# A hybrid attention layer on one core: other priorities and PSUM banks in the handover to the feed-forward, a shorter Newton step, and a last product in two column halves

## The chip, the cores and the metric

The kernel runs on one core of one Trainium2 chip. The metric is device time in microseconds (us) of one execution, from its start to its end. The engines are named as in the profile: PE is TensorE (matrix products and transposes), PEld its weight loads, DVE is VectorE, ACT is ScalarE, POOL is GpSimd and SP is SyncE, which here only issues transfers (DMA). PSUM is the memory into which PE writes its results; it has eight banks of 128 partitions by 512 fp32 columns.

## The reference

One decoder layer on 512 rows of 1024 columns, and a last normalisation, all in fp32:

```python
def rmsnorm(x, w):
    return x * lax.rsqrt(jnp.mean(x * x, axis=-1, keepdims=True) + EPS) * w

h = rmsnorm(x, norm1_w)
proj = h @ w_in                                  # split among three head groups
mix = concat(dilated_attention(...), gla(...), moba_attention(...))      # (512, 1024)
x = x + mix @ w_out
h2 = rmsnorm(x, norm2_w)
x = x + jnp.square(jax.nn.relu(h2 @ w_ff1)) @ w_ff2          # 1024 -> 4096 -> 1024
out = rmsnorm(x, final_norm_w)
```

The change begins where `x + mix @ w_out` has been formed and ends with the output.

## The kernel before

**Precision.** An fp32 matrix is held as a high part and a low part of a format that PE multiplies fast (`wh` and `wl` of a weight, `mh` and `ml` of `mix`, `yp` twice for the activations, `Ah` and `Al` for the hidden values). A product takes three matrix instructions: high by high, low by high, high by low. ACT makes a high part by a copy, DVE the low part by a subtraction. Weights arrive as `wraw` (512 KB a piece) and are split into `wh` and `wl`.

**Output projection** (`out_proj`). The rows are four tiles t = 0 to 3 of 128, the columns two halves of 512. Tiles 0 and 2 add up in the PSUM banks "mm", tiles 1 and 3 in "s" (tile name `ops`). As a half is done, `x2_out` adds it to `x` on DVE, ACT squares it with a running sum (`junk`, `ssq`), and DVE puts the sum into `m`. After the second half `inv_rms` works out 1/sqrt(m): ACT takes a logarithm and an exponential (both named `y` in the profile) and one Newton step on DVE refines the result (`tmp`, `tmp`, `y`). `y_out` scales each half (`y0`, shown as `y` of 128x512), PE transposes it into a bank (`yps`, four 128x128 transposes a half), and ACT or DVE copies it out with the norm's weights as scale (`yf`).

**Feed-forward** (`ffn`). The 4096 hidden columns are four chunks c. For each chunk the first layer (`f1...`) and the second (`f2...`) are each done as seven block products instead of eight (n = 0, 1, 3, 5, 2, 4, 6 in this order, in banks named X, Y and Z), whose operands are sums and differences of blocks: `y_parts` forms those of the activations (`ys`, then the high and low `yp`), `a_parts` those of the hidden values, and the weights' are formed by accumulating loads on POOL's queue or on DVE. The transposes of tiles 2 and 3 lie among the first chunk's products, since n = 0 and n = 1 need tiles 0 and 1 only.

**The end.** The last unit of work is the second layer of chunk 3, and its last product n = 6, for q = 0 (row tile t = 2) and then q = 1 (t = 3). `add` adds a product to `x`, `square_sum` and `final` normalise: the half that came last is written as `of` (DVE), the other half was multiplied with the final weights `fw` ahead of time on POOL (`xw`) and is only scaled by ACT. All output transfers are issued by SP.

**What sets the order.** The program is recorded by a planner (`Plan`). Each piece of work is a stream with a priority. The planner holds an estimated cost for every operation and picks again and again the operation that could start first, and among equals the stream with the lowest priority number; streams wait for each other's events (`wait`, `fire`) and for resources such as banks (`take`, `give`). Each engine then runs its operations in the order of these picks. All instructions are issued by one line, L129 of the kernel, so the profile tells them apart by tile names and not by lines.

Of the kernel before, what the change touches and what calls it, by code (L numbers as in the profile page):

```python
# [199 lines left out]
def hybrid_block_kernel(ctx: ExitStack, tc: tile.TileContext, xT_d, x_d, w0_d, wv_d, wqk_d, wo_d, w1_d, w2_d,  # L200
# [13 lines left out]
    def slot(name, dt=F32, shape=(128, 512)):  # L214
        return sp.tile(list(shape), dt, name=name, tag="slot", bufs=SLOTS)
# [20 lines left out]


    nw = consts.tile([128, 2, KT], F32)
    hsel = consts.tile([128, 4], F32)
    bav = consts.tile([128, 1], F32)  # L240
    ones = consts.tile([128, 128], F32)
# [696 lines left out]
        return slot(name, dt, (128, 2, 256))  # L938
    ssq = {}

    def square_sum(t, half):

        q = small("ssq", (128, 1))
        second = t in ssq
        if not second:
            ssq[t] = small("m", (128, 1))
        yield ACT.activation(slot("junk"), x3[t, half], AF.Square, accum_out=q)
        if second:
            yield ("wait", ("ssq0", t))
            plan.done.pop(("ssq0", t))  # L950
            yield DVE.scalar_tensor_tensor(ssq[t], q, 1.0 / D, ssq[t], op0=OP.mult, op1=OP.add)
            fire(("ssq", t))
        else:
            yield DVE.tensor_scalar(ssq[t], q, 1.0 / D, EPS, op0=OP.mult, op1=OP.add)
            fire(("ssq0", t))

    def inv_rms(t):
        yield ("wait", ("ssq", t))
        plan.done.pop(("ssq", t))
        m = ssq.pop(t)  # L960
        y, tmp = (small(x, (128, 1)) for x in ("y", "tmp"))
        yield from rsqrt(y, m, tmp)
        st["inv", t] = y

    def x2_out(t, half, acc, r):
        yield DVE.tensor_tensor(x3[t, half], acc, x3[t, half], op=OP.add)
        give(r)
        yield from square_sum(t, half)
        if half:
            yield from inv_rms(t)  # L970
            y = st.pop(("inv", t))
            for hf in range(2):
                spawn(y_out(t, hf, y), 1)

    def y_out(t, half, y):
        y0 = slot("y0")
        yield Any(DVE.tensor_scalar(y0, x3[t, half], y, None, op0=OP.mult), ACT.activation(y0, x3[t, half], AF.Copy, scale=y))
        yield ("take", "pt")
        pt = bank("pt", "yps")
        yield [PE.transpose(pt[:, i * 128:(i + 1) * 128], y0[:, i * 128:(i + 1) * 128], ident) for i in range(4)]  # L980
        ts = slice(t % 2 * 128, t % 2 * 128 + 128)
        ks = range(half * 4, half * 4 + 4)
        src = [pt[:, i * 128:(i + 1) * 128] for i in range(4)]
        if t % 2 == 0:
            yf[half, t // 2] = [new("yf") for _ in range(2)]
        else:
            yield ("wait", ("yf", t - 1, half))
        for i, k in enumerate(ks):
            out, scale = yf[half, t // 2][i // 2][:, i % 2, ts], nw[:, 1, k:k + 1]
            yield Any(ACT.activation(out, src[i], AF.Copy, scale=scale), DVE.tensor_scalar(out, src[i], scale, None, op0=OP.mult))  # L990
        give("pt")
        fire(("yf", t, half))

    def split(hi, lo, src):
# [48 lines left out]
    def out_proj():  # L1043
# [23 lines left out]

        def done(t, halves=(0, 1)):
            for half in halves:
                spawn(x2_out(t, half, accs[t][half], "mm" if t % 2 == 0 else "s"), 1)  # L1070

        for t in range(2):
            if t:
# [6 lines left out]
            done(t)  # L1080
        spawn(fetch_ff(), 4)
        spawn(cut_ff(), 3)
        spawn(y_parts(), 1)

        def let_go(i):
            give("big")
# [66 lines left out]
    def a_parts(c):  # L1153
# [43 lines left out]
        yield from urgent(6)  # L1197
        yield from parts_of(6, a22)

    def add(c, i, q, acc):  # L1200
        n, b_, _, targets = PRODUCTS[i]
        for blk, half in targets:
            t = 2 * blk + q
            if c == NC - 1 and n != 6:
                yield ("prio", 1.3 + i)
            yield DVE.tensor_tensor(x3[t, half], x3[t, half], acc, op=OP.subtract if half and b_ == "X" else OP.add)
            if c == NC - 1 and not any((blk, half) in p[3] for p in PRODUCTS[i + 1:]):
                spawn(square_sum(t, half), -1 if n == 6 else 0)
                if t in ssq:
                    spawn(final(t, half), -1 if n == 6 else 0)  # L1210
                else:
                    spawn(weighted(t, half), 9)
        if not any(p[1] == b_ for p in PRODUCTS[i + 1:]):
            give(TAGS[2][b_][q])
        fire(("read", (2, c), b_, q))
# [11 lines left out]
    def final(t, half):  # L1227
        yield from inv_rms(t)
        y = st.pop(("inv", t))
        yield ("wait", ("xw", t))  # L1230
        ts = slice(t * 128, (t + 1) * 128)
        a, b = (slice(h * 512, h * 512 + 512) for h in (half, 1 - half))
        for h, s in ((half, a), (1 - half, b)) if t < 2 else ((half, a),):
            of = slot("of")
            yield DVE.scalar_tensor_tensor(of, x3[t, h], y, fw[:, s], op0=OP.mult, op1=OP.mult)
            yield SP.dma_start(out_d[ts, s], of)
        if t < 2:
            return
        xw = st.pop(("xw", t))
        yield ACT.activation(xw, xw, AF.Copy, scale=y)  # L1240
        yield SP.dma_start(out_d[ts, b], xw)

    fw = None

    def load_fw():
        nonlocal fw
        yield ("wait", ("cut", (2, NC - 1), 1, 1))
        yield ("take", "big")
        fw = big("fw")
        yield SP.dma_start(fw, bass.AP(tensor=fw_d.tensor, offset=fw_d.offset, ap=[[0, 128], [1, 1024]]))  # L1250
        fire("fw")

    def ffn():
        def unit(u):
# [4 lines left out]
            for o, (n, b_, first_, _) in enumerate(PRODUCTS):  # L1259
                for q in range(2):  # L1260
# [3 lines left out]
                    else:  # L1264
                        yield ("wait", ("read", u, b_, q))
                        plan.done.pop(("read", u, b_, q))
                    acc = bk[b_, q]
                    for ip in range(2):
                        yield ("wait", ("Y", n, ip) if layer == 1 else ("A", c, n, ip))
                        yield ("wait", ("w", (u, n, ip)))  # L1270
# [2 lines left out]
                        for i in range(2):  # L1273
# [8 lines left out]
                            else:  # L1282
                                ws = slice(i * 512, i * 512 + 512)
                                ts = slice(q * 128, q * 128 + 128)
                                for j, (aa, ww) in enumerate(((ah, wh), (al, wh), (ah, wl))):
                                    ops.append(PE.matmul(acc, aa[:, i, ts], ww[:, ws], start=begin and j == 0, stop=end and j == 2,
                                                         skip_group_check=True))
                            yield ops
                        if q:
                            give_w()  # L1290
                            if layer == 2:
                                give("part")
                    last = u == units[-1] and n == 6
                    if layer == 1:
                        spawn(h_out(c, n, q, bk), 0)
                    else:
                        spawn(add(c, o, q, acc), -1 if last else 0)

        for u in units:
            if u == units[-1]:  # L1300
# [38 lines left out]
    def start():  # L1339
        yield ACT.dma_start(nw, nw_d)  # L1340
        yield SP.dma_start(xT[0], xT_d[0])
        fire(("x", 0))
        nc.scalar.preload_act_table_set("natural_log_exp_and_others")
        plan.clock["scalar"] += 1.3
        yield DVE.memset(ones, 1.0)
        yield DVE.memset(eps, EPS)
        for z in (rb, wa2, *oneh, alT):
            yield POOL.memset(z, 0.0)
        yield ("take", "mm")
        warm = bank("mm", "warm")  # L1350
        for _ in range(WARM):
            yield PE.matmul(warm[:, :128], ones, ones, start=True, stop=True)
        give("mm")
# [92 lines left out]
```

## Time and profile before

| | |
|---|---|
| median of 3 runs | 582.64 us (582.17 to 583.40) |
| the profiled execution | 583.02 us |
| its span, first to last instruction | 581.3 us, at a mean granted TensorE clock of 0.998 |
| PE busy | 566.5 us (97% of the span) |
| DVE, ACT, POOL busy | 448.1, 346.0 and 53.6 us |
| moved by DMA | 87.16 MB, 150 GB/s over the span |

A row of the profile's timeline gives the start in the span, the duration, the engine, the operation, what it writes and reads, its shape, and how many of its kind follow each other without another kind between them (x8). Brackets show the engine's idle time just before and the operation that ended it. PE's rows are pipelined: a product of 128x512 lasts 0.39 us, but the next one starts earlier than that, so work in a row is counted from start to start.

### The profile page before, as it was taken

The numbers are of one execution on the slowest core, as the hardware profiler recorded it, in microseconds if no ns is written. First come the engines' busy times: TensorE is split into PE (matmuls) and PEld (weight loads), VectorE is DVE, ScalarE is ACT, GpSimd is POOL, SyncE is SP. The second block draws the span as 40 slices with busy tenths as digits, with TensorE's granted clock in tenths as the row PEclk, the third lists the DMA queues.
The fourth block names the chain that finished last, engine by engine and source line by source line (L and its number), as shares of the span: only waits on it lengthen the run. The fifth ranks groups of instructions, "written<-read, shape, count | busy, mean of one in ns | idle before, by whom it ended". The sixth has DMA issues, their size and how long they took to land.

```text
span 581.3 us, 9334 instructions
## 1 busy us (share of the span) xinstructions
PE 566.5 (97%) x3549; PEld 486.3 (84%) x3549; DVE 448.1 (77%) x801; ACT 346.0 (60%) x597; POOL 53.6 (9%) x73
## 2 busy tenths in 40 slices
PE   8999999999999999999999999999999999999994
PEld 7967888768876778789988899988899888999883
DVE  5789976654787843659799797699985799958994
ACT  6653427646565752557795457865367764579643
POOL 4020000000000010011101102021020120012101
PEclk9999999999999999999999999999999999999999
DMA  8922232040424741378968737968369684395812
GB/s 293 392 79 74 73 110 83 26 145 8 135 77 126 272 113 32 112 222 188 240 195 168 182 110 166 304 112 224 100 143 292 147 164 163 109 217 109 146 38 108
DMA packets 27357, 87.16 MB, mean 150 GB/s; under 512 B 3360, under 2 KB 3402, under 8 KB 27312
## 3 DMA queue, kind: packets, MB, share of 16 engines
q1 hardware_dynamic: 20016, 61.42, 30.3%
q0 software_dynamic: 7152, 25.14, 23.8%
q8 instruction: 28, 0.46, 0.3%
q14 instruction: 17, 0.14, 0.1%
q10 hardware_dynamic: 144, 0.01, 0.0%
HBM read 84.42 MB, written 2.13 MB: 149 GB/s over the span
## 4 chain that ended last, share of the span: by engine, by line
PE 90%; DVE 5%; ACT 2%; issue 1%; DMA 1%; SPq 0%; DVEq 0%; ACTq 0%
PE f2X L129 15%; PE f1X L129 14%; PE qkps L129 12%; PE vps L129 8%; PE f2Z L129 7%; PE ops L129 7%; PE f1Z L129 7%; PE f2Y L129 4%; PE f1Y L129 3%; PE sps L129 3%; PE po L129 2%; PE ptp L129 2%; PE av L129 2%; DMA wraw<-in_w 1%; DVE yf L129 1%
## 5 line engine op out<-in xcount | busy, mean ns | idle before, releaser
L129 DVE TENSOR_TENSOR wl<-wraw,wh 128x1024 fp32r<-128x1024 f32 (+1 forms) x148 | 175.2, 1194 | 35.7 <-ACT wh L129 35.2
L129 ACT ACTIVATE wh<-wraw 128x1024 fp32r<-128x1024 f32 (+1 forms) x147 | 149.3, 1032 | 50.8 <-DMA wraw<-in_w 16.7
L129 PE MATMUL f1X<-yp,wh 128*128 128x256 f32 x512 | 92.6, 283 | 0.0
L129 POOL DMA_DIRECT2D wraw<-in_w x46 | 40.5, 978 | 470.8 <-DVE wl L129 229.5
L129 PEld LDWEIGHTS f1X<-yp,wh 128*128 128x128 f32 x512 | 80.2, 192 | 0.3
L129 PE MATMUL f1X<-yp,wl 128*128 128x256 f32 x256 | 72.7, 284 | 0.5 <-DVE wl L129 0.5
L129 PE MATMUL f2X<-wh,Ah 128*128 128x512 f32 x128 | 49.9, 390 | 0.0
L129 PE MATMUL f2X<-wh,Al 128*128 128x512 f32 x128 | 49.9, 390 | 0.0
L129 PE MATMUL f2X<-wl,Ah 128*128 128x512 f32 x128 | 49.8, 389 | 0.0
L129 PEld LDWEIGHTS f1X<-yp,wl 128*128 128x128 f32 x256 | 49.2, 192 | 0.7 <-DVE wl L129 0.7
L129 PE MATMUL f1Z<-yp,wh 128*128 128x256 f32 x256 | 46.7, 284 | 0.7 <-DVE yp L129 0.6
L129 ACT ACTIVATE h<-h 128x512 f32<-128x512 f32 x56 | 34.9, 626 | 11.0 <-DVE h L129 10.2
L129 PEld LDWEIGHTS f1Z<-yp,wh 128*128 128x128 f32 x256 | 40.1, 192 | 1.1 <-DVE yp L129 1.1
L129 PE MATMUL qkps<-xh,wh 128*128 128x512 f32 x96 | 40.9, 426 | 0.0
L129 PE MATMUL qkps<-xh,wl 128*128 128x512 f32 x96 | 37.6, 392 | 0.0
L129 PE MATMUL qkps<-xl,wh 128*128 128x512 f32 x96 | 37.6, 391 | 0.0
L129 ACT ACTIVATE Ah<-h 128x512 fp32r<-128x512 f32 x40 | 24.4, 621 | 21.3 <-DVE h L129 21.3
L129 ACT ACTIVATE P<-P,mn 128x512 f32<-128x512 f32 (+3 forms) x48 | 26.5, 554 | 17.6 <-DVE mn L129 17.6
L129 PE MATMUL f1Z<-yp,wl 128*128 128x256 f32 x128 | 36.3, 283 | 0.0
L129 DVE TENSOR_TENSOR Al<-h,Ah 128x512 fp32r<-128x512 f32 x40 | 27.1, 690 | 2.3 <-ACT Ah L129 2.1
L129 PEld LDWEIGHTS f2X<-wl,Ah 128*128 128x128 f32 x128 | 24.0, 188 | 5.0
L129 PEld LDWEIGHTS f2X<-wh,Al 128*128 128x128 f32 x128 | 24.0, 188 | 4.9
(225 smaller groups left out, 1200.9 us busy)
## 6 DMA issues: line engine op xcount, KB each, us to landing
wraw<-in_w SPq DMA_DIRECT2D x66, 512.0 KB, 4.5
wraw<-in_w POOLq DMA_DIRECT2D x46, 512.0 KB, 6.2
wraw<-in_wqk SPq DMA_DIRECT2D x12, 512.0 KB, 6.3
wraw<-in_wv SPq DMA_DIRECT2D x8, 512.0 KB, 6.4
wraw<-in_wo SPq DMA_DIRECT2D x8, 512.0 KB, 5.8
nb<-tab SPq DMA_DIRECT2D x12, 256.0 KB, 3.9
wraw<-in_w SPq DMA_DIRECT2D x8, 264.0 KB, 6.9
xT<-in_xT SPq DMA_DIRECT2D x8, 256.0 KB, 6.8
```

The source lines that it names most:

```text
L129: getattr(getattr(self.nc, op.eng), op.method)(*op.args, **op.kw)
```

## The change

Five edits. The shorter Newton step leaves out a factor of −0.5: it gives −2 times the result, and the norm's weights (`nw2`, a new 128x8 tile) and the final weights (`fw`, scaled on ACT after their load) carry −0.5 instead. Odd row tiles put their transposes into the banks "o" and "g", which nothing else holds at that time, and no longer into "pt". The streams of tiles 2 and 3 and of `y_parts` get higher priority (a lower number). The last product (n = 6, q = 1) is run as two column halves of 256, each added and squared by itself; tile 2's output waits until the second is added ("last x"). The last `xw` is sent from ACT's queue.

```diff
+    nw2 = consts.tile([128, KT], F32)
...
-    def square_sum(t, half):
+    def square_sum(t, half, cols=slice(0, 512), more=False):
...
-        yield ACT.activation(slot("junk"), x3[t, half], AF.Square, accum_out=q)
+        yield ACT.activation(slot("junk")[:, cols], x3[t, half][:, cols], AF.Square, accum_out=q)
...
-            fire(("ssq", t))
+            fire((("ssq0" if more else "ssq"), t))
...
-        yield from rsqrt(y, m, tmp)
+        yield ACT.activation(y, m, AF.Ln)
+        yield ACT.activation(y, y, AF.Exp, scale=-0.5)
+        yield DVE.scalar_tensor_tensor(tmp, y, y, m, op0=OP.mult, op1=OP.mult)
+        yield DVE.scalar_tensor_tensor(y, tmp, -3.0, y, op0=OP.add, op1=OP.mult)
...
-                spawn(y_out(t, hf, y), 1)
+                spawn(y_out(t, hf, y), 0.3 if t > 1 else 1)
...
-        yield ("take", "pt")
-        pt = bank("pt", "yps")
+        r = "og"[half] if t % 2 else "pt"
+        yield ("take", r)
+        pt = bank(r, "yps")
...
-            out, scale = yf[half, t // 2][i // 2][:, i % 2, ts], nw[:, 1, k:k + 1]
+            out, scale = yf[half, t // 2][i // 2][:, i % 2, ts], nw2[:, k:k + 1]
...
-        give("pt")
+        give(r)
...
-                spawn(x2_out(t, half, accs[t][half], "mm" if t % 2 == 0 else "s"), 1)
+                spawn(x2_out(t, half, accs[t][half], "mm" if t % 2 == 0 else "s"), 0.3 if t > 1 else 1)
...
-        spawn(y_parts(), 1)
+        spawn(y_parts(), 0.4)
...
+    def last_add(q, acc, cols, end):
+        t = 2 + q
+        yield DVE.tensor_tensor(x3[t, 0][:, cols], x3[t, 0][:, cols], acc[:, cols], op=OP.add)
+        spawn(square_sum(t, 0, cols, not end), -1)
+        if end:
+            spawn(final(t, 0), -1)
+            fire("last x")
...
+            if t == 2:
+                yield ("wait", "last x")
             yield DVE.scalar_tensor_tensor(of, x3[t, h], y, fw[:, s], op0=OP.mult, op1=OP.mult)
...
-        yield SP.dma_start(out_d[ts, b], xw)
+        yield (SP if t < 3 else ACT).dma_start(out_d[ts, b], xw)
...
+        yield ACT.activation(fw, fw, AF.Copy, scale=-0.5)
...
+                    halves = u == units[-1] and n == 6 and q == 1
...
+                    if halves:
+                        for cols in (slice(0, 256), slice(256, 512)):
+                            for ip in range(2):
+                                ah, al = A[c, n, ip]
+                                wh, wl = loaded[u, n, ip]
+                                yield [PE.matmul(acc[:, cols], aa[:, i, ts], ww[:, i * 512 + cols.start:i * 512 + cols.stop],
+                                                 start=False, stop=(ip + i == 2 and j == 2), skip_group_check=True)
+                                       for i in range(2) for j, (aa, ww) in enumerate(((ah, wh), (al, wh), (ah, wl)))]
+                            spawn(last_add(q, acc, cols, cols.start > 0), -1)
...
+        yield DVE.tensor_scalar(nw2, nw[:, 1], -0.5, None, op0=OP.mult)
```

On PE the change moves rows at two places only. The first is the handover, where the transposes (`yps`) of row tiles 0 and 1 stand among products of the output projection. Brackets name the semaphores on which a row waits. Before, in PE's row:

```order
L129 MATMUL yps<-cst,y_2633 128x128 [waits DVE_49,PE_49]
L129 MATMUL yps<-cst,y_2633 128x128 x3
L129 MATMUL yps<-cst,y_2634 128x128 [waits PE_49,Activation_49]
L129 MATMUL yps<-cst,y_2634 128x128 x3
L129 MATMUL ops<-wh,mh 128x512
L129 MATMUL ops<-wh,ml 128x512
L129 MATMUL ops<-wl,mh 128x512
L129 MATMUL yps<-cst,y_2645 128x128 [waits Activation_49]
L129 MATMUL yps<-cst,y_2645 128x128 x3
L129 MATMUL yps<-cst,y_2646 128x128 [waits DVE_49]
L129 MATMUL yps<-cst,y_2646 128x128 x3
```

And after the change, at the same place on PE:

```order
L129 MATMUL yps<-cst,y_2632 128x128 [waits DVE_49,PE_49]
L129 MATMUL yps<-cst,y_2632 128x128 x3
L129 MATMUL yps<-cst,y_2633 128x128 [waits PE_49,Activation_49]
L129 MATMUL yps<-cst,y_2633 128x128 x3
L129 MATMUL yps<-cst,y_2646 128x128 [waits DVE_49,PE_49]
L129 MATMUL yps<-cst,y_2646 128x128 x3
L129 MATMUL yps<-cst,y_2647 128x128 [waits Activation_49]
L129 MATMUL yps<-cst,y_2647 128x128 x3
L129 MATMUL ops<-wh,mh 128x512
```

The four groups of transposes now stand in one run, and the run begins three products earlier in PE's row than before. The transposes of tiles 2 and 3 keep their places on PE.

On DVE the rows behind the last `yf` of tile 3 change places (`wl` a weight's low part, `ys` a difference of activation blocks, `h` a block of the hidden layer, `yp` a low part for PE, `Al` one of the hidden values). Before:

```order
L129 TENSOR_TENSOR wl<-wraw,wh 128x1024 [waits DMASW5_49,Activation_49]
L129 TENSOR_TENSOR wl<-wraw,wh 128x1024 [waits DMAHW7_49,Activation_49]
L129 TENSOR_TENSOR ys<-yf 128x512 [waits DVE_49]
L129 TENSOR_TENSOR wl<-wraw,wh 128x1024 [waits DMAHW0_49,Activation_49]
L129 TENSOR_TENSOR h<-h,f1Y 128x512 [waits PE_49]
L129 TENSOR_TENSOR ys<-yf 128x512 [waits DVE_49]
L129 TENSOR_TENSOR yp<-ys,yp 128x512 [waits Activation_49] x2
L129 TENSOR_TENSOR h<-h,f1Y 128x512 [waits PE_49]
L129 TENSOR_TENSOR ys<-ys,yf 128x512 [waits DVE_49]
```

After, the same stretch of DVE:

```order
L129 TENSOR_TENSOR wl<-wraw,wh 128x1024 [waits DMASW5_49,Activation_49]
L129 TENSOR_TENSOR ys<-yf 128x512 [waits DVE_49] x2
L129 TENSOR_TENSOR wl<-wraw,wh 128x1024 [waits DMAHW7_49,Activation_49]
L129 TENSOR_TENSOR h<-h,f1Y 128x512 [waits PE_49]
L129 TENSOR_TENSOR yp<-ys,yp 128x512 [waits Activation_49] x2
L129 TENSOR_TENSOR ys<-ys,yf 128x512 [waits DVE_49]
L129 TENSOR_TENSOR wl<-wraw,wh 128x1024 [waits DMAHW0_49]
L129 TENSOR_TENSOR h<-h,f1Y 128x512 [waits PE_49]
```

One of three `wl` rows, that of the queue DMAHW0, moved from ahead of the `yp` pair to behind it, and the two `ys` rows stand together.

The third place is DVE's last rows (`x_...` the half of a row tile to which the last product is added: tile 2, then tile 3). Before:

```order
L129 SCALAR_TENSOR_TENSOR of<-x_2290,y,fw 128x512 [waits DVE_49]
L129 TENSOR_TENSOR x_2297<-x_2297,f2X 128x512 [waits PE_49]
L129 SCALAR_TENSOR_TENSOR m<-ssq,m 128x1 [waits Activation_49]
L129 TENSOR_TENSOR tmp<-y 128x1 [waits Activation_49]
L129 SCALAR_TENSOR_TENSOR tmp<-tmp,m 128x1 [waits DVE_49]
L129 SCALAR_TENSOR_TENSOR y<-tmp,y 128x1 [waits DVE_49]
L129 SCALAR_TENSOR_TENSOR of<-x_2297,y,fw 128x512 [waits DVE_49]
```

After:

```order
L129 TENSOR_TENSOR x_2299<-x_2299,f2X 128x256 [waits PE_49]
L129 TENSOR_TENSOR x_2299<-x_2299,f2X 128x256
L129 SCALAR_TENSOR_TENSOR of<-x_2292,y,fw 128x512 [waits DVE_49]
L129 SCALAR_TENSOR_TENSOR m<-ssq,m 128x1 [waits Activation_49]
L129 SCALAR_TENSOR_TENSOR m<-ssq,m 128x1 [waits DVE_49,Activation_49]
L129 SCALAR_TENSOR_TENSOR tmp<-y,m 128x1 [waits DVE_49,Activation_49]
L129 SCALAR_TENSOR_TENSOR y<-tmp,y 128x1 [waits DVE_49]
L129 SCALAR_TENSOR_TENSOR of<-x_2299,y,fw 128x512 [waits DVE_49]
```

Tile 3's sum comes in two halves, the wait for PE stands ahead of the first of them (its count is that of the last of the 24 products), and tile 2's output `of` moved from ahead of it to behind it.

More of the change, by code (lines that the diff above doesn't have):

```diff
@@ L1287, in unit @@
                                                          skip_group_check=True))
-                            yield ops
+                            if not halves:
+                                yield ops
                         if q:
@@ L1292, in unit @@
                                 give("part")
-                    last = u == units[-1] and n == 6
-                    if layer == 1:
+                    if halves:
[7 more added lines that the diff above has]
+                            spawn(last_add(q, acc, cols, cols.start > 0), -1)
+                    elif layer == 1:
                         spawn(h_out(c, n, q, bk), 0)
                     else:
-                        spawn(add(c, o, q, acc), -1 if last else 0)
+                        spawn(add(c, o, q, acc), -1 if u == units[-1] and n == 6 else 0)
         for u in units:
```

## Prediction

> **What bounds the kernel now.** I read the table of busy times by stretches first, then the waits of TensorE (PE), and last the rows of time around each wait and of the tail.
>
> ```profile
> 270.00:276.00 6.00, 5.88 (x49) 5.68 (x49) 6.00 (x10) 5.17 (x10) 0.87 (x1) 1.00 0.67 122
> 276.00:290.00 14.00, 14.00 (x118) 14.00 (x119) 10.67 (x15) 10.56 (x17) 2.67 (x3) 1.00 1.01 247
> 300.00:573.00 273.00, 273.00 (x1680) 246.62 (x1678) 232.24 (x289) 167.31 (x234) 34.61 (x38) 1.00 0.64 159
> ```
>
> ```profile
> PE yps L129 <- DVE y L129: 1.1, 1, 1.1
> PE f1Z L129 <- DVE yp L129: 0.6, 1, 0.6
> PE yps L129 <- DVE yf L129: 0.6, 1, 0.6
> PE f1X L129 <- DVE wl L129: 0.5, 1, 0.5
> PE yps L129 <- ACT yf L129: 0.5, 1, 0.5
> ```
>
> The first table's columns are the stretch, its length, the busy time of PE, its weight loads, DVE, ACT and POOL with their counts, the granted clock, the DMA share and GB/s. PE is the bound. From 300 to 573 us it is busy all 273.00 us, so nothing that happens in that stretch can be won by a better order; only an earlier arrival at 300 counts, and it counts in full as long as nothing there runs dry. The five waits are all of PE's after 200 us, 3.3 us together, and all lie in the handover. PE's last product (quoted with the tail below) ends at 573.17; the 8.1 us from there to the span's end at 581.3 are the other place that the change touches. So the sum has two parts, the handover and the tail.
>
> **Part 1: transposes of row tiles 0 and 1 (banks "o" and "g", priorities).**
>
> ```profile
> 233.04 1.04 PE L129 MATMUL yps<-cst,y 128*128 128x128 f32 x8
> 233.83 0.47 PE L129 MATMUL ops<-wh,mh 128*128 128x512 f32 x1
> ...
> 235.27 0.66 PE L129 MATMUL yps<-cst,y 128*128 128x128 f32 x4 [0.50 <-ACT yf L129]
> 236.51 0.66 PE L129 MATMUL yps<-cst,y 128*128 128x128 f32 x4 [0.58 <-DVE yf L129]
> 236.92 0.48 PE L129 MATMUL ops<-wh,mh 128*128 128x512 f32 x1
> ```
>
> Tile 0 takes both "pt" banks, so tile 1's transposes wait until ACT and DVE have emptied them (yf). With banks of their own all 16 transposes stand in one run. Eight took 233.83 − 233.04 = 0.79, so sixteen take 1.6, then three products 0.23 apart (the rows of 251.54 and 251.77 below): the product of 236.92 starts at 233.04 + 1.6 + 0.7 = 235.35. That is 1.55 us earlier. The run starts three products (0.7 us) earlier, when the scaled tiles have to be ready; the shorter Newton step and tile 1's own place make up for most of it. I take 1.55; the low end is 0.84, if only the second gap closes (1.24 from 235.27 to 236.51, where four transposes take 0.40), the high end 1.75.
>
> **Part 2: the Newton step, two small DVE operations for three.**
>
> ```profile
> 251.20 0.16 DVE L129 SCALAR_TENSOR_TENSOR tmp<-tmp,m 128x1 f32<-128x1 f32 x1
> 251.39 0.16 DVE L129 SCALAR_TENSOR_TENSOR y<-tmp,y 128x1 f32<-128x1 f32 x1
> ```
>
> ```profile
> 251.54 0.39 PE L129 MATMUL ops<-wh,ml 128*128 128x512 f32 x1
> 251.77 0.39 PE L129 MATMUL ops<-wl,mh 128*128 128x512 f32 x1
> 252.22 1.06 PE L129 MATMUL yps<-cst,y 128*128 128x128 f32 x8
> ...
> 259.39 0.28 PE L129 MATMUL f1X<-yp,wl 128*128 128x256 f32 x1
> 260.75 1.06 PE L129 MATMUL yps<-cst,y 128*128 128x128 f32 x8 [1.08 <-DVE y L129]
> ```
>
> ```profile
> 257.73 1.22 DVE L129 TENSOR_TENSOR wl<-wraw,wh 128x1024 fp32r<-128x1024 f32 x1 [0.80 <-ACT wh L129]
> ```
>
> Dependent small operations start 0.19 apart, so each chain is 0.19 shorter. Tile 2: PE loses 0.45 − 0.23 (a product's spacing) = 0.22 ahead of its transposes; 0.19 of it goes (0 to 0.22). Tile 3: PE loses 1.36 − 0.12 = 1.24 (products of 256 columns stand 0.12 apart: a pair's row below is 0.40 long, a single one's 0.28). The change's order leaves the 1.22 us subtraction (wl) between the two squares' sums of tile 3 and leaves its transposes at their place on PE, so the priority does not shorten this; 0.20 goes and about 1.04 stays (0 to 1.24). The operation that makes the scaled norm weights (128x8, at the start) and the scaling of the final weights on ACT (128x1024, near 532 us) I cost at nothing: the first lies on DVE while the first matrix is on its way, the second in a stretch where ACT is busy 167.31 of 273.00 us. If that cover were gone, they would cost up to the 1.22 us of the subtraction above, the nearest row in size, and the first far less.
>
> **Part 3: the parts of the second activations (y_parts at 0.4).**
>
> ```profile
> 268.84 0.28 PE L129 MATMUL f1Z<-yp,wh 128*128 128x256 f32 x1
> 269.71 0.39 PE L129 MATMUL f1Z<-yp,wh 128*128 128x256 f32 x1 [0.58 <-DVE yp L129]
> ...
> 275.44 0.78 PE L129 MATMUL f1Z<-yp,wh 128*128 128x256 f32 x2
> ```
>
> ```profile
> 268.96 1.47 DVE L129 TENSOR_TENSOR yp<-ys,yp 128x512 fp32r<-128x512 f32 x2
> ...
> 273.89 0.68 DVE L129 TENSOR_TENSOR Al<-h,Ah 128x512 fp32r<-128x512 f32 x1
> ```
>
> Ahead of the first low part (yp) one weight subtraction fewer stands on DVE (two where three were): 1.22 us by the row above, against 0.75 that PE loses at 269.71 (0.87 from start to start, where such products stand 0.12 apart). That wait vanishes. But DVE is busy 6.00 of 6.00 us here, so what was moved behind yp comes before the next product's parts. Only an Al (0.68 by its row, 0.6 until the next one starts) leaves their path, and PE comes 0.75 earlier: the row of 275.44, two products that take 0.78 where the pair takes 0.40 elsewhere and so lose up to 0.38, of which I put 0.28 down to the wait, then loses about 0.43. Net 0.75 + 0.28 − 0.43 = 0.60 (0.2 to 1.03).
>
> ```profile
> 294.52 0.40 PE L129 MATMUL f1X<-yp,wh 128*128 128x256 f32 x2
> 295.46 0.39 PE L129 MATMUL f1X<-yp,wl 128*128 128x256 f32 x1 [0.53 <-DVE wl L129]
> ```
>
> The last wait, 0.94 − 0.24 = 0.70 lost on a weight's low part, stands behind DVE's turn through Al, h and wl. By the new order DVE gets there about 0.3 earlier against PE: 0.30 (0 to 0.70).
>
> Handover: 1.55 + 0.19 + 0.20 + 0.60 + 0.30 = 2.84 us.
>
> **Part 4: the tail.**
>
> ```profile
> 572.78 0.39 PE L129 MATMUL f2X<-wl,Ah 128*128 128x512 f32 x1
> 573.21 0.75 DVE L129 SCALAR_TENSOR_TENSOR of<-x,y,fw 128x512 f32<-128x512 f32 x1
> 573.88 0.68 DVE L129 TENSOR_TENSOR x<-x,f2X 128x512 f32<-128x512 f32 x1
> 574.59 0.63 ACT L129 ACTIVATE junk<-x 128x512 f32<-128x512 f32 x1 [0.60 <-DVE x L129]
> 575.13 0.19 ACT L129 ACTIVATION_READ_ACCUMULATOR junk<-x 128x1 f32 x1
> ...
> 575.54 0.20 ACT L129 ACTIVATE y<-m 128x1 f32<-128x1 f32 x1 [0.23 <-DVE m L129]
> ...
> 576.65 0.72 ACT L129 ACTIVATE xw<-xw,y 128x512 f32<-128x512 f32 x1 [0.68 <-DVE y L129]
> 577.38 0.33 SPq L129 DMA_DIRECT2D out<-of  x1
> 577.80 0.38 SPq L129 DMA_DIRECT2D out<-xw  x1
> DMA to landing us min/median/max: 2.0/2.0/2.3
> ```
>
> Before: PE ends at 573.17, but DVE is inside tile 2's output (of) and adds only at 573.88; that is 0.7 lost. After, tile 2's output waits for "last x". Twenty-four products of half width are 0.12 apart instead of twelve 0.227 apart, so PE ends 0.15 later, at 573.32. The order puts one wait on PE ahead of both half adds, for the last of the 24, so the halves do not overlap PE: adds at 573.35 and 573.69 (half of 0.68 plus a fixed part, estimated 0.41 each, 0.34 apart), squares at 573.79 and 574.26, the read of their sum done at 574.78 where it was 575.32. Before, the logarithm began 0.22 behind that read (575.54). After, it could at 575.00, but tile 2's xw stands ahead of it on ACT (about 0.63 to the next start, 574.68 to 575.31). From the logarithm to the last xw lie 1.11 us (575.54 to 576.65), less one Newton operation 0.92: xw starts at 576.23 and it and of end at 576.95, where they ended at 577.37. Both transfers then start at 576.95, where they started at 577.38 and 577.80. Before, they landed 0.72 apart (577.38 + 2.0, 577.80 + 2.3) though issued 0.42 apart: they share what carries them. So the second lands at 576.95 + 2.0 + 0.72 = 579.67 where it was 580.10: 0.43. If the second issue is free and shares nothing, 576.95 + 2.3 = 579.25, 0.85; if the ACT issue is slower than SP's, 0.2.
>
> The Trainium skill, DMA: Bandwidth & Descriptors, "Issuing engines are not separate DMA queues", says that transfers from several issuing engines end up on the same 16 engines and that a second issuer saves only issue time. It speaks against the larger value; by it the tail is 0.43, without it 0.85, and the 0.72 between two landings goes its way.
>
> **Sum.** 2.84 + 0.43 = 3.27 us. The profiled execution took 583.02 us (span 581.3 and 1.7 around it) and would take 579.75. It lies 0.38 above the median of 582.64, so the median after is 579.4.
>
> **Rivals.**
> - *The halves do overlap PE.* Then the first add and square run under the second half's products, and one square (0.47) leaves the chain: 3.74 in all, 578.9. Against it stands the order: the second add has no wait of its own, the first waits for PE's last product. Chance 0.05. The Trainium skill, PSUM — Partial Sum Buffer, "PSUM bank collisions raise a hardware error", says that two engines must be kept apart by bank, not by address, and the two halves are one bank; no run here shows it.
> - *DVE takes the handover's gain back.* PE comes earlier, DVE is full (6.00 of 6.00) and DMA too (share 1.01 from 276 to 290), so PE waits at 275 for parts that come no earlier. Taken in full, parts 1 to 3 lose all but the 0.30 of the last wait: 0.30 + 0.43 = 0.73, 581.9. By half, 580.7. For it speaks that the later waits are DVE's; against it that DVE's own start (the yf of tile 3) hangs on PE and moves with it. Chance 0.06 in full, 0.10 by half.
> - *Slower: a late weight.* The POOL queue's accumulating loads are released by other engines' rows and share a full DMA with SP's:
>
> ```profile
> 277.31 1.23 DVE L129 TENSOR_TENSOR wl<-wraw,wh 128x1024 fp32r<-128x1024 f32 x1 [0.33 <-ACT wh L129]
> 283.00 0.40 PE L129 MATMUL f1X<-yp,wh 128*128 128x256 f32 x2
> ```
>
> This subtraction ends at 278.54 and PE uses it at 283.00: 4.46 of slack. A load that came 4.46 + 3.27 + 1.2 = 8.9 us late would make the kernel slower than before by 0.2%, since each us past the slack costs one. At 10 us late the time is 584.9. Nothing in 300 to 573 us, where PE takes weights from the same queues for 273 us, was ever late. Chance 0.03.
> - *The change does not do what it says:* the rows keep waiting although they stand elsewhere, say since both engines' sequences slip together. The 16 transposes stand in one run in the order and have banks that nothing else holds, so I give it 0.01: 582.6.
>
> **Numbers.** Forecast 0.75, the rivals as above. 0.2% (1.2 us) is about what a measurement of this kernel tells from no change. Faster: 0.75 + 0.05 + 0.10 = 0.90; within 0.2%: 0.06 + 0.01 = 0.07; slower: 0.03. The range goes from the upper ends of parts 1, 3 and 4 (0.2 + 0.43 + 0.40 + 0.42 more, 577.9) to the half-taken gain with a tail of 0.2 (580.9).
>
> **What would show it.** Right: one row of 16 transposes near 233 us with no wait inside; a wait of about 1 us ahead of tile 3's; no wait at the first f1Z low part and one of about 0.4 us one product later; a last add 0.03 us behind PE's end; two outputs issued together, landing 0.7 us apart. Wrong: a first add ahead of PE's last product (first rival); new PE waits between 270 and 300 us that sum to over 2 us (second); any PE wait on a weight in 300 to 573 us (third).

## The result and the profile after

The changed kernel takes 579.58 us (median of 7 runs, 578.71 to 581.27), the kernel before 582.77 us (7 runs, 582.17 to 583.77). The ratio is 0.9946, 95% interval 0.9931 to 0.9962: 3.2 us faster, 2.2 to 4.0. The forecast was 579.4. One execution of a later kernel (f1) took 1130.7 us, nearly twice the others, and nothing on record shows why; f1's time and ratio below are those of its other four.

PE's waits behind 200 us, in the profiled execution after (579.58 us, span 577.8). A row says who waited for whom, then the total in us, how many times, and the longest:

```profile
PE yps L129 <- DVE y L129: 0.8, 1, 0.8
PE f1Z L129 <- DVE yp L129: 0.3, 1, 0.3
PE f1X L129 <- DVE wl L129: 0.2, 1, 0.2
```

Three waits are left of five, 1.3 us where there were 3.3. The timeline of PE in the handover shows where they were:

```profile
231.62 1.91 PE L129 MATMUL yps<-cst,y 128*128 128x128 f32 x16
233.29 0.47 PE L129 MATMUL ops<-wh,mh 128*128 128x512 f32 x1
...
249.51 0.39 PE L129 MATMUL ops<-wl,mh 128*128 128x512 f32 x1
249.83 1.07 PE L129 MATMUL yps<-cst,y 128*128 128x128 f32 x8
...
258.12 1.09 PE L129 MATMUL yps<-cst,y 128*128 128x128 f32 x8 [0.84 <-DVE y L129]
...
292.01 0.38 PE L129 MATMUL f1X<-yp,wl 128*128 128x256 f32 x1 [0.24 <-DVE wl L129]
```

Sixteen transposes stand in one row, 1.67 from start to the next product. Ahead of tile 2's they lose 0.32 − 0.23 = 0.09 where it was 0.22; tile 3's still wait 0.84 (1.08 before).

The tail, all engines:

```profile
569.99 0.28 PE L129 MATMUL f2X<-wl,Ah 128*128 128x256 f32 x1
570.31 0.75 DVE L129 TENSOR_TENSOR x<-x,f2X 128x256 f32<-128x256 f32 x2 [0.31 <-PE f2X L129]
570.76 0.42 ACT L129 ACTIVATE junk<-x 128x256 f32<-128x256 f32 x1 [1.21 <-DVE x L129]
...
571.49 0.18 ACT L129 ACTIVATION_READ_ACCUMULATOR junk<-x 128x1 f32 x1
571.58 0.71 ACT L129 ACTIVATE xw<-xw,y 128x512 f32<-128x512 f32 x1
...
572.19 0.19 ACT L129 ACTIVATE y<-m 128x1 f32<-128x1 f32 x1
...
573.15 0.72 ACT L129 ACTIVATE xw<-xw,y 128x512 f32<-128x512 f32 x1 [0.54 <-DVE y L129]
573.87 0.33 SPq L129 DMA_DIRECT2D out<-of  x1
573.90 0.37 ACTq L129 DMA_DIRECT2D out<-xw  x1
DMA to landing us min/median/max: 2.0/2.1/2.7
```

Both half additions start behind PE's last product (ends 570.27, additions from 570.31): the halves do not overlap PE. The two last transfers start 0.03 apart; the first takes 2.3 us to land and the second 2.7, so they land 0.4 apart.

One loss stands in no term of the sum. It lies in the second layer of the first chunk, on PE, on DVE and on ACT:

```profile
330.43 0.39 PE L129 MATMUL f2X<-wh,Al 128*128 128x512 f32 x1
330.90 0.50 PE L129 MATMUL f2X<-wl,Ah 128*128 128x512 f32 x1
```

```profile
329.62 1.23 DVE L129 TENSOR_TENSOR wl<-wraw,wh 128x1024 fp32r<-128x1024 f32 x1 [2.61 <-ACT wh L129]
```

```profile
328.53 4.85 ACT L129 ACTIVATE wh<-wraw 128x1024 fp32r<-128x1024 f32 x5 [3.60 <-DMA wraw<-in_w]
```

The product at 330.90 starts 0.47 behind the one before it, where 0.23 is usual, and the one behind it 0.34. It needs the low part that DVE finishes at 330.85, which waited for ACT's high part, which waited 3.60 us for a load. In the kernel before, ACT waited for the same load, and PE did not:

```profile
331.05 4.85 ACT L129 ACTIVATE wh<-wraw 128x1024 fp32r<-128x1024 f32 x5 [2.70 <-DMA wraw<-in_w]
```

**One table for all kernels.** Single executions differ by up to 1.9 us before the change even begins (last section), so stages are compared, not spans. The stages, from starts in the timelines (and, for D, the last landing): A, from the 101st product of the output projection (229.86 us before) to the first f2X product (299.64); B, from there to the first f2X product of the second chunk (378.06); C, from there to the end of PE's last product; D, from there to the last landing. In us:

| kernel | A | B | C | D | sum |
|---|---|---|---|---|---|
| before | 69.78 | 78.42 | 195.11 | 6.94 | 350.25 |
| changed | 67.05 | 78.84 | 195.26 | 6.28 | 347.44 |
| banks alone (e1) | 68.18 | 78.42 | 195.11 | 6.92 | 348.64 |
| Newton alone (e2) | 69.27 | 78.42 | 195.11 | 6.67 | 349.46 |
| priorities alone (e3) | 68.92 | 79.01 | 195.11 | 6.92 | 349.96 |
| new end alone (e4) | 69.77 | 78.42 | 195.26 | 6.43 | 349.87 |
| last product whole (f1) | 67.05 | 78.98 | 195.11 | 6.37 | 347.51 |
| last xw on SP (f2) | 67.05 | 78.65 | 195.26 | 6.33 | 347.29 |
| transposes later (f3) | 66.93 | 78.42 | 195.26 | 6.28 | 346.89 |
| bank of its own (f4) | 67.06 | 78.68 | 195.26 | 5.90 | 346.90 |
| split held back (g1) | 65.66 | 78.77 | 195.26 | 6.29 | 345.98 |
| g1 and f4 (g2) | 65.65 | 78.74 | 195.26 | 5.90 | 345.55 |
| f3 and f4 (g3) | 66.91 | 78.73 | 195.26 | 5.91 | 346.80 |
| half loads (g4) | 67.04 | 78.42 | 195.26 | 6.29 | 347.00 |

A, C and D repeat to 0.05 us wherever the stage's code is the same. B is 78.42 in the four kernels without the new priorities, however early PE arrives (e1 comes 1.60 us earlier). In the nine that have them, with the loads whole, it lies between 78.42 and 79.01.

Of the kernels built on the changed one, only g1 and g2 stand clearly apart from it in measured time. What the others gain or lose against it is read from the stages of one execution each.

### The profile page after: what moved, and what is told of

Read it like the earlier page. It is cut to its first block, busy times and chain, and to the rows that moved or that the text cites. A ratio compares the mean times of both kernels' runs of the same rounds, so it can differ in the third digit from the quotient of the medians.

```text
span 577.8 us, 9359 instructions
## 1 busy us (share of the span) xinstructions
PE 566.3 (98%) x3561; PEld 487.3 (84%) x3561; DVE 446.6 (77%) x795; ACT 346.7 (60%) x601; POOL 53.6 (9%) x73
## 4 chain that ended last, share of the span: by engine, by line
PE 85%; DVE 7%; ACT 3%; DMA 2%; issue 1%; ACTq 0%; DVEq 0%
PE f1X L129 13%; PE f2X L129 12%; PE qkps L129 12%; PE vps L129 8%; PE ops L129 7%; PE f1Z L129 7%; PE f2Z L129 6%; PE f1Y L129 3%; PE f2Y L129 3%; PE sps L129 3%; DMA wraw<-in_w 2%; PE po L129 2%; PE ptp L129 2%; PE av L129 2%; DVE wl L129 2%
## 5 line engine op out<-in xcount | busy, mean ns | idle before, releaser
L129 PE MATMUL f2X<-wl,Ah 128*128 128x512 f32 (+1 forms) x132 | 50.6, 384 | 0.1
L129 PE MATMUL f2X<-wh,Ah 128*128 128x512 f32 (+1 forms) x132 | 50.6, 383 | 0.0
L129 PE MATMUL f2X<-wh,Al 128*128 128x512 f32 (+1 forms) x132 | 50.6, 383 | 0.0
L129 PEld LDWEIGHTS f2X<-wh,Ah 128*128 128x128 f32 x132 | 24.8, 188 | 4.8
```

Source lines behind the costliest of these rows:

```text
L129: getattr(getattr(self.nc, op.eng), op.method)(*op.args, **op.kw)
```

## Experiments

Each was run against the kernel before, and the ratio is to that, also where the edit starts from the changed kernel.

### The four parts alone

e1, the banks:

```diff
-        yield ("take", "pt")
-        pt = bank("pt", "yps")
+        r = "og"[half] if t % 2 else "pt"
+        yield ("take", r)
+        pt = bank(r, "yps")
```

> The kernel before with one edit alone: odd row tiles put their transposes into the banks o and g. Theory (the terms add up as in the sum): one run of 16 transposes, about 1.4 us gained there, and the time falls by 1.2 to 1.7 us, since DVE's later work hangs on tile 3's transposes and moves with PE. Rival (DVE takes it back): the waits at f1Z and f1X between 265 and 297 us grow by what was gained; the time falls by less than 0.5 us.

581.21 us, ratio 0.9971 (0.9959 to 0.9983). Stage A is 1.60 shorter, the others are as before. Its PE waits:

```profile
PE yps L129 <- DVE y L129: 1.0, 1, 1.0
PE f1Z L129 <- DVE yp L129: 0.6, 1, 0.6
PE f1X L129 <- DVE wl L129: 0.5, 1, 0.5
```

The two later ones are the same size as before. Nothing was taken back: DVE's row is set off by tile 3's transposes and moves with PE. The gain lies within the 1.2 to 1.7 expected, and the rival falls.

e2, the shorter Newton step with its scaled weights:

```diff
-        yield from rsqrt(y, m, tmp)
+        yield ACT.activation(y, m, AF.Ln)
+        yield ACT.activation(y, y, AF.Exp, scale=-0.5)
+        yield DVE.scalar_tensor_tensor(tmp, y, y, m, op0=OP.mult, op1=OP.mult)
+        yield DVE.scalar_tensor_tensor(y, tmp, -3.0, y, op0=OP.add, op1=OP.mult)
...
+        yield ACT.activation(fw, fw, AF.Copy, scale=-0.5)
```

> The kernel before with the shorter Newton step alone (and the norm weights scaled by -0.5 that belong to it). Theory: each chain of tiles 2 and 3 is 0.2 us shorter and so is the tail's: 0.2 + 0.2 + 0.2, 0.4 to 0.7 us less; the two added scaling operations show no wait of another engine. Rival: the scaling of the final weights on ACT or the one at the start costs what the step gains; no difference.

582.01 us, ratio 0.9984 (0.9975 to 0.9992). A is 0.51 shorter, D 0.27: 0.78, a little more than expected, and at other places. Only 0.14 and 0.05 of A come at tiles 2 and 3, where 0.2 each was expected. The other 0.32 come at the transposes of tiles 0 and 1, of which eight now stand three products earlier in PE's order. D gains about 0.14 twice, since here tile 2's output still stands ahead of tile 3's addition. That D moves by 0.27 and C by nothing shows that the added scaling on ACT is covered.

e3, the priorities:

```diff
-                spawn(y_out(t, hf, y), 1)
+                spawn(y_out(t, hf, y), 0.3 if t > 1 else 1)
...
-        spawn(y_parts(), 1)
+        spawn(y_parts(), 0.4)
```

> The kernel before with the new priorities alone. PE's order is the same as before, only DVE and ACT rows change places. Theory: the wait at the first low part of f1Z goes (0.7) and the one of f1Z's next product grows a little, the last one at f1X shrinks by 0.3: 0.5 to 1.0 us less. Rival: priorities only move the waits from one product to the next: under 0.3 us.

582.55 us, ratio 0.999 (0.9979 to 1.0002): no difference that can be told from zero, where the theory had 0.5 to 1.0. The rival's size was right, its place was not. A is 0.86 shorter, as the theory had it; B is 0.59 longer. Among PE's waits stands one that the kernel before did not have:

```profile
PE f2X L129 <- DVE wl L129: 0.3, 1, 0.3
```

It is the loss near 331 us. So the priorities gain in the handover and give two thirds back 35 us later, in a stage in which PE was busy without a gap before. The three priority numbers were not tried one by one.

e4, the new end (the diff of `last_add`, of the column halves, of "last x" and of the last transfer, as shown above, without the Newton step):

> The kernel before with the new end alone: the last product in two column halves, tile 2's output behind the last addition, the last xw on ACT's queue; Newton step as before. Theory: PE's last product ends 0.15 later, the first half's addition starts only behind it, and the last landing comes 0.2 to 0.4 us earlier; the time falls by that. Rival (the halves overlap PE): the first addition starts some 1.4 us ahead of PE's end, and the gain is 0.7 us or more.

582.57 us, ratio 0.9995 (0.9986 to 1.0004). C is 0.15 longer, D 0.51 shorter: 0.36, within what the theory said and too little to show in the time of a whole run. The halves do not overlap PE, so the rival falls: the additions begin at 573.01, PE's last product ends at 572.98:

```profile
572.70 0.28 PE L129 MATMUL f2X<-wl,Ah 128*128 128x256 f32 x1
573.01 0.75 DVE L129 TENSOR_TENSOR x<-x,f2X 128x256 f32<-128x256 f32 x2 [0.18 <-PE f2X L129]
```

### The tail taken apart

f1, the last product whole again, in the changed kernel:

```diff
-                    halves = u == units[-1] and n == 6 and q == 1
+                    halves = False
...
+                    elif u == units[-1] and n == 6 and q == 1:
+                        spawn(last_add(q, acc, slice(0, 512), True), -1)
```

> The changed kernel with the last product whole again (12 products of 512 columns, one addition, one square); tile 2's output still waits for the addition, the rest as changed. Theory (the halves share a bank and do not overlap PE): PE ends 0.15 us earlier and the sum of squares is complete about 1.47 us behind PE's end instead of 1.40, so the end moves by -0.1 us: nothing measurable. Rival (the halves are what gains in the tail): 0.4 us or more slower than the changed kernel.

579.86 us (four executions), ratio 0.9949 (0.9935 to 0.9963), against 0.9946 for the changed kernel: no difference. C + D is 201.48 where the changed kernel has 201.54. The column halves gain nothing; they cost 0.06. C + D is still 0.57 shorter than before. Of that 0.14 is the Newton step's and 0.05 the last transfer's (f2); the rest is left to tile 2's output behind the addition, which was not run by itself.

f2, the last transfer on SP's queue:

```diff
-        yield (SP if t < 3 else ACT).dma_start(out_d[ts, b], xw)
+        yield SP.dma_start(out_d[ts, b], xw)
```

> The changed kernel with the last xw sent from SP's queue, as before. Theory (the two last transfers share what carries them): issued 0.4 us later but landing within 0.1 us of where it lands now, about 2.7 us behind the end of of; no measurable difference. Rival (a queue of its own is worth the issue time): the last landing comes 0.4 us later.

580.45 us, ratio 0.996 (0.9945 to 0.9975), which cannot be told from the changed kernel's. D is 6.33 where it was 6.28, and the rival falls. Its last rows:

```profile
574.14 0.33 SPq L129 DMA_DIRECT2D out<-of  x1
574.56 0.38 SPq L129 DMA_DIRECT2D out<-xw  x1
DMA to landing us min/median/max: 2.0/2.0/2.3
```

Issued 0.42 apart, the two take 2.0 and 2.3 to land; issued 0.03 apart, 2.3 and 2.7. Issuing the second 0.39 earlier brings its landing only 0.05 forward. That is the rule that the prediction took from the Trainium skill (DMA: Bandwidth & Descriptors, "Issuing engines are not separate DMA queues"), and the trace agrees with it.

f4, a bank of its own for the last product's first half:

```diff
+                        yield ("take", "mm")
+                        fresh = bank("mm", "fresh")
+                        early = slice(0, 256)
+                        spawn(early_add(q, acc, early), -1)
...
-                                yield [PE.matmul(acc[:, cols], ...
-                                                 start=False, ...
+                                yield [PE.matmul((acc if cols.start else fresh)[:, cols], ...
+                                                 start=(not cols.start and ip + i + j == 0), ...
...
-                            spawn(last_add(q, acc, cols, cols.start > 0), -1)
+                            spawn(last_add(q, acc if cols.start else fresh, cols, cols.start > 0), -1)
```

> The changed kernel with the last product's first column half in a bank of its own; what stands in the old bank for it is added to x while PE still works, one more addition. Theory: the first half's addition and square now run under the second half's products, the sum of squares is complete 0.4 to 0.5 us earlier behind PE's end, and the last landing comes 0.4 to 0.5 us earlier. Rival (the square was covered anyway, or ACT's xw of tile 2 takes the room): under 0.2 us.

579.27 us, ratio 0.9936 (0.9923 to 0.9949). D falls from 6.28 to 5.90. The first half's addition and square now lie ahead of PE's end at 570.37:

```profile
568.97 0.42 DVE L129 TENSOR_TENSOR x<-x,fresh 128x256 f32<-128x256 f32 x1 [0.75 <-PE fresh L129]
569.43 0.42 ACT L129 ACTIVATE junk<-x 128x256 f32<-128x256 f32 x1 [0.45 <-DVE x L129]
...
570.88 0.42 ACT L129 ACTIVATE junk<-x 128x256 f32<-128x256 f32 x1 [0.62 <-DVE x L129]
570.95 0.75 DVE L129 SCALAR_TENSOR_TENSOR of<-x,y,fw 128x512 f32<-128x512 f32 x1
571.20 0.19 ACT L129 ACTIVATION_READ_ACCUMULATOR junk<-x 128x1 f32 x1
571.30 0.71 ACT L129 ACTIVATE xw<-xw,y 128x512 f32<-128x512 f32 x1
571.62 0.15 DVE L129 SCALAR_TENSOR_TENSOR m<-ssq,m 128x1 f32<-128x1 f32 x1
```

With one bank the program's wait ahead of the first half's addition is for the last of all 24 products; with two it is for the first half's own. So here the halves do what they read like only when they are two banks. Whether the chip would allow the early read from a shared bank, no run shows. The gain is 0.38, just under the 0.4 to 0.5 expected. The rows show what holds it: `m` starts 0.42 behind the read of the square's sum, as tile 2's `of` occupies DVE, where it starts 0.22 behind it in the kernel before (575.35 and 575.13). Tile 2's `xw` on ACT adds about 0.1 ahead of the logarithm.

### Tile 3's wait

f3, its transposes later in PE's order:

```diff
+        if t == 3:
+            fire(("later", half), plan.now + 1.1)
+            yield ("wait", ("later", half))
         yield ("take", r)
```

> The changed kernel with the planner told that tile 3's scaled halves are ready 1.1 us later, which puts its transposes six products later into PE's order. Theory (the place on PE makes the wait of 0.84 us there, but DVE is full behind it): that wait goes or shrinks to 0.2, and the f1Z and f1X waits grow by most of it; the time falls by 0 to 0.4 us. Rival: the wait is PE's own loss and the whole 0.8 us is gained.

579.3 us, ratio 0.9939 (0.9925 to 0.9952). The wait ahead of the transposes is gone, and the one at f1Z has grown from 0.3 to 0.7:

```profile
PE f1Z L129 <- DVE yp L129: 0.7, 2, 0.5
PE f1X L129 <- DVE wl L129: 0.2, 1, 0.2
```

A is only 0.12 shorter than in the changed kernel: PE's place made the wait, and DVE took it back. Another 0.42 came in B, where this execution had no loss near 331 us; g3 tells whether that is owed to the edit.

g1, one weight's split held back:

```diff
+                    if u == units[0] and n == 3 and ip == 0:
+                        yield ("wait", "x2 done")
                     yield from parts((u, n, ip), B[u, n, ip])
...
             yield from inv_rms(t)
+            if t == 3:
+                fire("x2 done")
```

> The changed kernel with one weight's split (the first of product n = 3) held back until tile 3's 1/rms is known, so that neither its wh on ACT nor its wl on DVE stands between tile 3's two squares. Theory (the wait of 0.84 us ahead of tile 3's transposes is made by this split): the chain is 1.2 to 1.5 us shorter, that wait shrinks to 0.2 or less and, since DVE's later work starts earlier too, the waits at f1Z do not grow: 0.7 to 1.0 us gained by 300 us. Rival (given back later, by a late weight at f2X near 331 us, as the priorities alone showed): PE is early at 300 us but loses half or more of it at 331 us; under 0.4 us in all.

578.16 us, ratio 0.9924 (0.9911 to 0.9936). A is 65.66, 1.39 shorter than in the changed kernel and more than expected; B is as there. In the changed kernel the weight's split stands between tile 3's two squares, its high part on ACT and its low part on DVE ahead of `m`:

```profile
254.25 1.04 ACT L129 ACTIVATE wh<-wraw 128x1024 fp32r<-128x1024 f32 x1
255.20 0.61 ACT L129 ACTIVATE junk<-x 128x512 f32<-128x512 f32 x1
```

```profile
255.33 1.23 DVE L129 TENSOR_TENSOR wl<-wraw,wh 128x1024 fp32r<-128x1024 f32 x1 [0.80 <-ACT wh L129]
256.47 0.15 DVE L129 SCALAR_TENSOR_TENSOR m<-ssq,m 128x1 f32<-128x1 f32 x1
```

In g1 the second square on ACT follows the first, and the weight's high part comes behind the chain:

```profile
253.93 0.63 ACT L129 ACTIVATE junk<-x 128x512 f32<-128x512 f32 x1 [1.02 <-DVE x L129]
...
254.56 0.62 ACT L129 ACTIVATE junk<-x 128x512 f32<-128x512 f32 x1
...
255.84 1.04 ACT L129 ACTIVATE wh<-wraw 128x1024 fp32r<-128x1024 f32 x1
```

Of PE's waits behind 200 us one is left:

```profile
PE f1X L129 <- DVE wl L129: 0.2, 1, 0.2
```

About 0.75 came at the transposes, and 0.64 more at f1Z, where DVE, off to an earlier start, is no longer late. The rival falls: B loses 0.35, no more than in the changed kernel. f3 and g1 together show which resource it was: moving PE's row alone won 0.12, shortening the chain in front of DVE's work won 1.39.

g2 and g3 put the bank of its own beside each.

> The run before this one (the held-back split) together with the last product's first half in a bank of its own. Theory (the two gains lie at different places of PE's chain and add up): the handover's gain as there, and 0.4 us in the tail. Rival: only the larger of the two.

> Tile 3's transposes six products later together with the bank of its own, both as run alone. Theory (terms add up): 0.5 + 0.4 us below the changed kernel. Rival: what the later transposes gained beyond 0.2 us was chance in how the loads near 331 us met, and only 0.4 to 0.6 us are gained.

g2: 578.12 us, ratio 0.9923 (0.991 to 0.9935). In the stages both gains are there (A 65.65, D 5.90; the sum is 1.89 below the changed kernel's), but the times of g1 and g2 cannot be told apart. g3: 579.13 us, ratio 0.9942 (0.9929 to 0.9954); A 66.91, B 78.73, D 5.91. With the same handover as f3, B has 0.31 of loss: f3's clean B was no effect of the edit. The sum is 0.64 below the changed kernel's, near the rival's 0.4 to 0.6 and not the theory's 0.9.

### The loss near 331 us

g4 halves the two accumulating loads that make the weights of that product:

```diff
-        yield from plus(t, (1, 0))
+        part = slice(0, 512 if u == units[1] else 1024)
+        yield POOL.dma_start(t[:, part], quad_d(u, (1, 0), ip)[:, part], accum_op=OP.add)
```

> The changed kernel, but the two accumulating loads that make the weights of the second layer's last product in the first chunk add only half of their columns, 256 KB instead of 512 KB each; half of these sums is left out, so the output differs. Theory (the new loss of 0.36 us near 331 us is the second of these loads landing late): it lands 1.5 us or more earlier, PE loses nothing at 331 us, 0.3 to 0.4 us less. Rival (ACT or DVE is late with the split there, whatever the load does): PE still loses 0.3 us there.

579.38 us, ratio 0.9943 (0.9929 to 0.9956), which cannot be told from the changed kernel's. B is 78.42, to the hundredth what it was before the change. ACT's row of splits starts at 324.78 where it started at 328.53:

```profile
324.78 3.98 ACT L129 ACTIVATE wh<-wraw 128x1024 fp32r<-128x1024 f32 x4 [3.36 <-DMA wraw<-in_w]
```

So the late load made the loss: with it early, neither ACT nor DVE is late. In the changed kernel POOL issues it here:

```profile
317.78 0.88 POOL L129 DMA_DIRECT2D wraw<-in_w  x1 [0.62 <-DVE wl L129]
```

The row before the change is the same but for its start, 321.53. There it lands 9.4 us after its issue, in the changed kernel 10.6. To compare all kernels, the starts of this row and of ACT's high part are counted from the first f2X product, the beginning of B:

| kernel | A shorter by | POOL issues the load | ACT's high part starts | B above 78.42 |
|---|---|---|---|---|
| before, e1, e2, e4 | 0, 1.60, 0.51, 0.01 | 21.89 | 30.43 to 31.46 | 0 |
| half loads (g4) | 2.74 | 21.60 | 28.37 | 0 |
| f3 | 2.85 | 21.60 | 31.98 | 0 |
| f2 | 2.73 | 21.60 | 32.17 | 0.23 |
| f4 | 2.72 | 21.60 | 32.19 | 0.26 |
| g3 | 2.87 | 21.60 | 32.26 | 0.31 |
| g2 | 4.13 | 21.60 | 32.28 | 0.32 |
| g1 | 4.12 | 21.60 | 32.33 | 0.35 |
| changed | 2.73 | 21.60 | 32.35 | 0.42 |
| f1 | 2.73 | 21.60 | 32.53 | 0.56 |
| e3 | 0.86 | 21.60 | 32.56 | 0.59 |

The loss follows the load and not PE's arrival. Beyond about 32.0 a load that is later by some tenths costs PE as many tenths. How early PE comes does not decide it: e1 comes 1.60 earlier and loses nothing, e3 0.86 earlier and loses most, g1 4.12 earlier and loses less than e3.

What brings the load there is the priorities: e3 has them alone, and e1, e2 and e4, without them, have no loss. In every kernel with them and whole loads the load takes 10.3 to 10.9 us to land, in the four without them 8.4 to 9.5. In those with them the next load on SP's queue is issued 2.2 us behind it, and 4.0 in the four without. That the two loads share the engines and slow each other fits this but was not tried; the few tenths by which kernels with the same order differ are not explained.

## Why the prediction was right

The sum was 3.27; the stages give 350.25 − 347.44 = 2.81. Term by term, from the starts of the same products in both timelines:

| step | forecast | measured |
|---|---|---|
| transposes of tiles 0 and 1 | 1.55 | 1.51 |
| tile 2's chain | 0.19 | 0.14 |
| tile 3's chain | 0.20 | 0.22 |
| f1Z, gained and lost again | 0.60 | 0.83 − 0.28 = 0.55 |
| f1X, last wait | 0.30 | 0.30 |
| handover (A) | 2.84 | 2.73 |
| loss near 331 us (B) | 0 | −0.42 |
| tail (C and D) | 0.43 | −0.15 + 0.66 = 0.51 |

- The handover held in each term, since each was a gap in PE's row with the releaser beside it. The two places where the forecast held back were right: tile 3's wait stayed (0.84 of 1.08), as the split stayed between the two squares, and g1 shows that it was the split; and the f1Z gain was partly lost one product later. The row of 16 transposes without a wait inside refutes the fourth rival.
- The step that failed is the premise that nothing in 300 to 573 us runs dry, which put the loss there at 0. A weight came late and cost 0.42. The earlier arrival itself does count in full: e1 comes 1.60 earlier and B stays 78.42. It is the priorities, which parts 1 and 3 counted as a gain alone, that also delay an accumulating load against PE. The third rival had the mechanism, a late accumulating load, and expected it at another product, 283 us, and far larger. Its sign, a PE wait on a weight in 300 to 573 us, came. The cover of loads that come later was not looked at.
- The second rival, that DVE takes the gain back, is refuted by e1 as a whole; the part of it that is true is the 0.28 at f1Z, which was in the sum, and f3. (By half it gives 580.64; the prediction wrote 580.7, and nothing hangs on it.)
- The tail's working held up to the transfers: the halves did not overlap (first rival refuted by the additions' starts, f1 and f4), and PE ended 0.15 later. The last landing came 2.69 behind the first of the two issues (2.72 forecast), but not as forecast: the two land 0.4 apart and not 0.7, and the first takes 2.3 and not 2.0. That these two misses cancel is luck. The Newton step saved 0.14 there and not 0.19, as its remaining pair of operations takes 0.45 from start to `of` (before, three took 0.59).
- The operations that the prediction put at nothing cost nothing that the stages show: C is 195.11 in e2 with the scaling of the final weights, and A's first product starts between 228.60 and 230.21 us in the kernels with the one on DVE, between 228.89 and 230.53 in those without.
- That the profiled execution agreed to 0.2 us with the forecast (579.58 and 579.75) is partly luck: its 101st product of the output projection starts 0.74 us earlier than in the execution before, which no part of the change does, and this hid the 0.42. The median of seven runs, 3.2 below, has an interval of 2.2 to 4.0 and holds both 2.81 and 3.27.

## What to carry to other kernels

In this kernel each gap in the row of the engine that bounds the time could be priced by itself, with its releaser. Parts run alone add up only nearly: banks, Newton step and priorities shorten the handover by 1.60, 0.51 and 0.86, 2.97 in all, and together by 2.73, since two of them gain at the same transposes. A wait went when the chain in front of the releasing engine got shorter (g1), and came back at f1Z when only the waiting row was put elsewhere (f3).

A stage without any gap can still lose: before an order is changed, look up by how much each load lands ahead of its use, also far behind the place that is changed, and what the new order issues beside it. Splitting a product so that its first part can be read early took a bank for each part here.

## What was not expected of the hardware

The first microseconds differ from execution to execution: the 101st product of the output projection started between 228.60 and 230.53 us in the fourteen profiles, with the same rows ahead of it but for one small operation. Between the kernel before and the changed one the difference begins with the second piece of weights, for which ACT waits. The kernel before:

```profile
8.17 0.64 ACT L129 ACTIVATE wh<-wraw 128x528 fp32r<-128x528 f32 x1 [1.60 <-DMA wraw<-in_w]
```

The changed kernel:

```profile
7.27 0.65 ACT L129 ACTIVATE wh<-wraw 128x528 fp32r<-128x528 f32 x1 [0.80 <-DMA wraw<-in_w]
```

Both loads were issued at 2.12 us. Why one lands later is not known. A difference of half a microsecond between two kernels can't be read from one span each; counted from a product behind the start, the same stage repeats to 0.05 us.
